# An encoder kernel's opening rewritten: gain row spread by a matmul, dummy products, a hand-pinned order of the first norm tiles

## The chip, the cores and the metric

One core of a Trainium2 chip runs the whole program. The metric is the device time of one execution in microseconds; lower is better. Three runs of the kernel before gave 1115.28, 1116.11 and 1116.93 us (median 1116.11 us).

## The reference, cut to what matters

One encoder layer is applied to two sequences of 512 tokens, each with 16 shared meta tokens ahead of it, in float32. What matters here is its beginning:

```python
hn = _rms(h, attn_norm_g[i])            # x * rsqrt(mean(x*x) + EPS) * g, over 1024 channels
z = hn @ w_in[i]
c_val, c_gate, cq, ckv, k_rope = jnp.split(z, ...)      # 512, 512, 256, 256, 32 columns
u = c_val * jax.nn.sigmoid(c_gate)
u = _depthwise_conv(u, conv_dw_w[i], conv_dw_b[i])      # 31 taps, 512 channels
u = jax.nn.silu(_layernorm(u, conv_ln_g[i], conv_ln_b[i]))
...
# o: attention of 8 heads over latent queries and keys
h = h + jnp.concatenate([u, o], axis=-1) @ w_out[i]
hf = _rms(h, ffn_norm_g[i])
h = h + (jax.nn.silu(hf @ w_gate[i]) * (hf @ w_up[i])) @ w_down[i]
return _rms(h, final_norm_g)[:, N_META:]
```

## The kernel before, in words

Both sequences share one matrix of 1040 token columns: 512 of the first sequence, 16 meta tokens, 512 of the second. The tokens come in nine tiles (`TOK`): tiles 0 to 3 and 5 to 8 of 128 tokens, tile 4 of the 16 meta tokens.

Every large product is made of three passes over operands split into a high and a low part (`fp32r`): high by high, high by low, low by high, added in one PSUM bank (`mm3`, L151). So each weight tile of 128 x 1024 (`pair`) is loaded into a buffer `raw` (two buffers), cast to its high part on ScalarE (L134), and its low part is made by a subtraction on GpSimd (L137). Only when that subtraction is done can `raw` be loaded again.

A norm tile (`norm_tile`) goes this way: the load of `x` (L230, four buffers); the sum of squares on ScalarE (L175); the factor `rs` in two small operations on GpSimd (L176, L177); `xn = x * rs * gain` on VectorE (L237), where `gain` is a tile of 128 equal rows that one transfer of 512 KB has filled (L168); eight transposes on TensorE (L240); the high part `hn_h` by a cast on ScalarE (L141) and the low part `hn_l` by a subtraction on VectorE (L142).

The input product is done by channel blocks of 128. For the convolution's block c (`g0` to `g3`) a gate tile and a value tile of weights are needed: `glu_gate` makes a sigmoid into a `slots` row (L271), `glu_val` multiplies into `U` (L279, L281). Block 0 is done in four column groups (`FIRST`: 256, 272, 256 and 256 columns) as the norm tiles come; the others follow in three groups (`GROUPS`: 512, 272 and 256), in the order of `STEPS`: `g1 c0 g2 c1 g3 c2 q c3 k r n`. A `c` is the convolution of a block: some taps are done by ScalarE and GpSimd (L305, L307), the rest is two chains of operations on VectorE (L322 to L343). `q` and `k` are the latent queries and keys (sums of squares L385, L380, L406, L407), `r` the rotary keys (L436, L437; its table `rope_t` is loaded in L428), `n` the norm of the latent keys (L414, L418). Attention follows, then the output product, the norm and the feed-forward part.

The order on each engine is written out by a scheduler ahead of the run: it gives each engine, in a simulated time, the instruction that is ready and stands earliest in the program. On the chip each engine's instructions start in that order. `tc.keep_in_program_order(ins)` binds an instruction behind the one that stands just before it in the program on the same engine; this is an order of issue, not a wait for the end. The kernel before uses it for some operations of the feed-forward part alone. TensorE's results go to four one-bank buffers (`bank`, tag `t`) and two two-bank buffers (tag `s`).

Of the kernel before, what the change touches and what calls it, by code (L numbers as in the profile page):

```python
# [12 lines left out]
F32 = mybir.dt.float32  # L13
F32R = mybir.dt.float32r
AF = mybir.ActivationFunctionType
# [54 lines left out]
AHEAD = 3  # L70
STEPS = "g1 c0 g2 c1 g3 c2 q c3 k r n"
V_LATE = 1
# [28 lines left out]
def encoder_kernel(ctx: ExitStack, tc: tile.TileContext, x, meta, gains, w_in, w_kr, small, conv_w, wq, wk, wv,  # L101
# [10 lines left out]
    def name(p):  # L112
        n_tile[0] += 1
        return f"{p}_{n_tile[0]}"
# [12 lines left out]
    def pair(src, pool=None, tag="pair", bufs=4):  # L127

        pool = pool or stream
        raw = stream.tile([P, 1024], F32, tag="raw", bufs=2, name=name("raw"))  # L130
        nc.sync.dma_start(raw, src)
        both = pool.tile([P, 2, 1024], F32R, tag=tag, bufs=bufs, name=name("wp"))
        hi, lo = both[:, 0, :], both[:, 1, :]
        nc.scalar.copy(hi, raw)  # L134
        for a in range(0, 1024, LO_W):
            a = slice(a, a + LO_W)
            nc.gpsimd.tensor_sub(lo[:, a], raw[:, a], hi[:, a].bitcast(F32))  # L137
        return hi, lo

    def split(hi, lo, src, src_lo=None):  # L140
        nc.scalar.copy(hi, src)  # L141
        nc.vector.tensor_sub(lo, src_lo if src_lo is not None else src, hi.bitcast(F32))  # L142
# [18 lines left out]
    nc.vector.memset(mhalf, -0.5)  # L161
    nc.scalar.activation(tiny[:, 1:2], ones, AF.Square)
    gq, gkv = sm[:, 0:2], sm[:, 2:4]
    conv_b = sm[:, 4:8]
    ln_g, ln_b = sm[:, 8:12], sm[:, 12:16]
    def gain(i):
        g = const.tile([P, D], F32, tag="gain", bufs=1, name=name("gain"))
        nc.sync.dma_start(g, gains[i:i + 1, :].partition_broadcast(P))  # L168
        return g

    def rms_scale(src, rows, junk):
# [26 lines left out]
             "k": lambda c: [2 * NCH + KL, 2 * NCH + KL + 1], "r": lambda c: [-1]}  # L198
    for step in ("g0 " + STEPS).split():
# [32 lines left out]

    def norm_tile(t, xt):
        col, rows = TOK[t]
        xn = start.tile([P, D], F32, tag="xn", bufs=3, name=name("xn"))
        rs = rms_scale(xt[:rows], rows, start.tile([P, D], F32, tag="junk", bufs=1, name=name("junk")))
        nc.vector.scalar_tensor_tensor(xn[:rows], xt[:rows], rs[:rows], g_attn[:rows], ALU.mult, ALU.mult)  # L237
        pt = psum.tile([P, KD, 128], F32, tag="s", bufs=2, name=name("px"))
        for k in range(KD):
            nc.tensor.transpose(pt[:, k, :rows], xn[:rows, k * 128:(k + 1) * 128], ident[:rows, :rows])  # L240
        split(hn_h[:, :, col:col + rows], hn_l[:, :, col:col + rows], pt[:, :, :rows])

# [3 lines left out]

    def in_proj(i, c0, n):
        pt = bank()
        wh, wl = loaded[i]
        k128 = [slice(k * 128, (k + 1) * 128) for k in range(KD)]  # L250
# [17 lines left out]

    def glu_gate(c, c0, n):
        pg = in_proj(first_of[f"g{c}"], c0, n)  # L270
        nc.scalar.activation(slot(c % 2)[:, c0:c0 + n], pg[:, :n], AF.Sigmoid)  # L271

    def glu_val(c, c0, n):
        sig = slot(c % 2)
        pv = in_proj(first_of[f"g{c}"] + 1, c0, n)
        if True:
# [91 lines left out]
    start_pool.__exit__(None, None, None)  # L368
# [55 lines left out]
    def rope_keys(_):  # L424

        load_w_in(first_of["r"] + AHEAD)
        rope_t = taps.tile([P, NCOL], F32, name="rope_t")
        nc.sync.dma_start(rope_t, rope_k)  # L428
        wb = loaded[first_of["r"]]
# [572 lines left out]

    def in_order(ins):
        tc.keep_in_program_order(ins)

    def g_sums(p, j):
# [321 lines left out]
```

## Time and profile before

| | |
|---|---|
| median of three runs | 1116.11 us (1115.28 to 1116.93) |
| the profiled execution | 1116.52 us, its span 1114.7 us |
| TensorE busy | 1073.9 us (96%) |
| VectorE busy | 835.2 us (75%) |
| ScalarE busy | 500.0 us (45%) |
| GpSimd busy | 472.8 us (42%) |
| DMA | 147.06 MB, mean 132 GB/s |

The shares are averages over the whole span. For a change in the first part, the tables of short stretches, the instructions in order of time and the chain of work that ended last are to be read: they say which engine is full in which stretch, and what the next step waited for. In the rows of instructions in order of time the columns are the start in us, the length in us, engine, line, operation, output and inputs, and how many were merged; in brackets stands the idle time of that engine ahead of it and what ended it.

### The profile page before, as it was taken

The numbers are of one execution on the slowest core, as the hardware profiler recorded it, in microseconds if no ns is written. First come the engines' busy times: TensorE is split into PE (matmuls) and PEld (weight loads), VectorE is DVE, ScalarE is ACT, GpSimd is POOL, SyncE is SP. The second block draws the span as 40 slices with busy tenths as digits, with TensorE's granted clock in tenths as the row PEclk, the third lists the DMA queues.
The fourth block names the chain that finished last, engine by engine and source line by source line (L and its number), as shares of the span: only waits on it lengthen the run. The fifth ranks groups of instructions, "written<-read, shape, count | busy, mean of one in ns | idle before, by whom it ended". The sixth has DMA issues, their size and how long they took to land.

```text
span 1114.7 us, 15902 instructions
## 1 busy us (share of the span) xinstructions
PE 1073.9 (96%) x5874; PEld 928.4 (83%) x5874; DVE 835.2 (75%) x1197; ACT 500.0 (45%) x832; POOL 472.8 (42%) x409
## 2 busy tenths in 40 slices
PE   4999999899998999979999999999999999999997
PEld 4998887788887999968888888888888888888886
DVE  5599997788887555999768767876787596557643
ACT  6455434777785453552232223233323354433331
POOL 6389735654553231576555544554555200000012
PEclk9999999999999999989999999999999999999999
DMA  8211111110100412324354345435543899865503
GB/s 280 71 55 38 48 39 60 39 33 26 39 21 19 171 41 93 114 95 158 135 201 158 119 164 191 168 103 191 187 152 106 277 335 348 288 204 174 182 26 129
DMA packets 71421, 147.06 MB, mean 132 GB/s; under 512 B 6944, under 2 KB 29728, under 8 KB 71344
## 3 DMA queue, kind: packets, MB, share of 16 engines
q1 hardware_dynamic: 71344, 146.06, 38.4%
q8 instruction: 46, 0.75, 0.3%
q14 instruction: 31, 0.25, 0.1%
HBM read 105.92 MB, written 40.11 MB: 131 GB/s over the span
## 4 chain that ended last, share of the span: by engine, by line
PE 77%; DVE 16%; ACT 3%; DMA 1%; issue 1%; POOL 1%; SPq 0%; POOLq 0%; ACTq 0%; DVEq 0%
PE pt L151 58%; PE ps L151 13%; DVE ps L329 3%; DVE ps L337 3%; PE pt L645 3%; PE pt L615 2%; DVE pacc L339 1%; DVE hf L879 1%; PE px L240 1%; DVE wc L964 1%; ACT p L587 1%; DVE act_l L898 1%; DMA raw<-in_w_in_dram 1%; DVE tt L946 0%; DVE cq_l L142 0%
## 5 line engine op out<-in xcount | busy, mean ns | idle before, releaser
L151 PE MATMUL pt<-act_h,wc 128*128 128x512 f32 (+1 forms) x552 | 176.2, 382 | 0.1
L964 POOL TENSOR_TENSOR wc<-tt,wc 128x512 fp32r<-128x512 f32 x84 | 117.7, 1417 | 106.6 <-ACT wc L962 60.0
L151 PE MATMUL pt<-hn_h,wp 128*128 128x256 f32 (+2 forms) x576 | 132.4, 323 | 1.1 <-ACT hn_h L141 1.1
L151 PEld LDWEIGHTS pt<-act_h,wc 128*128 128x128 f32 x552 | 103.4, 190 | 19.8 <-issue 0.3
L176 POOL TENSOR_SCALAR ms<-ms 128x1 f32<-128x1 f32 (+1 forms) x24 | 13.2, 552 | 249.9 <-ACT re L175 213.8
L151 PE MATMUL pt<-act_l,wc 128*128 128x512 f32 (+1 forms) x276 | 105.6, 383 | 3.7 <-DVE act_l L898 3.4
L151 PEld LDWEIGHTS pt<-hn_h,wp 128*128 128x128 f32 x576 | 97.0, 191 | 10.1 <-ACT hn_h L141 1.5
L962 ACT CAST wc<-tt 128x512 fp32r<-128x512 f32 x88 | 51.3, 617 | 118.6 <-PE pt L151 115.3
L1133 DVE TENSOR_TENSOR re<-re,re 128x1024 fp32r<-128x1024 f32 x53 | 63.9, 1222 | 45.0 <-ACT re L1132 43.5
L151 PE MATMUL pt<-hn_l,wp 128*128 128x256 f32 (+2 forms) x288 | 93.5, 325 | 0.0
L137 POOL TENSOR_TENSOR wp<-raw,wp 128x1024 fp32r<-128x1024 f32 x28 | 69.3, 2476 | 54.4 <-ACT wp L134 54.3
L1132 ACT CAST re<-re 128x1024 fp32r<-128x1024 f32 x53 | 54.9, 1054 | 67.9 <-PE pt L151 24.7
L151 PE MATMUL pt<-re 128*128 128x512 f32 x360 | 84.0, 389 | 0.0
L151 PEld LDWEIGHTS pt<-re 128*128 128x128 f32 x360 | 67.6, 188 | 14.0
L590 POOL TENSOR_SCALAR p<-p,sst 128x512 f32<-128x512 f32 x64 | 44.3, 698 | 68.8 <-DVE sst L588 60.9
L151 PE MATMUL pt<-wp,act_h 128*128 128x256 f32 x384 | 71.4, 285 | 1.6 <-DVE h L842 1.5
L151 PEld LDWEIGHTS pt<-act_l,wc 128*128 128x128 f32 x276 | 52.4, 190 | 13.9 <-DVE act_l L898 3.6
L151 PE MATMUL ps<-re 128*128 128x512 f32 x276 | 63.9, 389 | 0.0
L964 POOL TENSOR_TENSOR wc<-raw,wc 128x512 fp32r<-128x512 f32 x30 | 40.3, 1357 | 52.6 <-ACT wc L962 52.6
L151 PEld LDWEIGHTS pt<-wp,act_h 128*128 128x128 f32 x384 | 60.1, 192 | 2.1 <-DVE h L842 1.7
L307 POOL TENSOR_TENSOR pacc<-pacc,prod 128x512 f32<-128x512 f32 x43 | 58.3, 1356 | 7.0 <-ACT prod L305 4.3
L151 PEld LDWEIGHTS ps<-re 128*128 128x128 f32 x276 | 51.8, 188 | 10.7
(283 smaller groups left out, 2889.5 us busy)
## 6 DMA issues: line engine op xcount, KB each, us to landing
raw<-in_w_gate_dram SPq DMA_DIRECT2D x22, 512.0 KB, 4.3
hf<-in_w_down_dram SPq DMA_DIRECT2D x44, 256.0 KB, 4.0
re<-in_w_down_dram SPq DMA_DIRECT2D x31, 256.0 KB, 5.3
raw<-in_w_in_dram SPq DMA_DIRECT2D x12, 512.0 KB, 3.9
slots<-in_w_up_dram SPq DMA_DIRECT2D x11, 512.0 KB, 3.5
h<-in_w_up_dram SPq DMA_DIRECT2D x11, 512.0 KB, 5.6
d_t1t<-hf SPq DMA_DIRECT2D x22, 256.0 KB, 5.5
d_t4t<-hf SPq DMA_DIRECT2D x22, 256.0 KB, 2.5
```

Of the source, the lines that this page charges most:

```text
L137: nc.gpsimd.tensor_sub(lo[:, a], raw[:, a], hi[:, a].bitcast(F32))
L151: nc.tensor.matmul(out_ap, lhsT=w_, rhs=m_, start=first and i + j == 0, stop=last and i == n - 1 and j == 2)
L307: nc.gpsimd.tensor_add(acc, acc, to)
L329: nc.vector.scalar_tensor_tensor(a_, half_win(c, 0, i, HS + 1), k, a_, ALU.mult, ALU.add)
L337: nc.vector.scalar_tensor_tensor(m_, both[:, :, i:i + HS], k, m_, ALU.mult, ALU.add)
L590: nc.gpsimd.tensor_scalar(pr[:, real], pr[:, real], st[:, 2, t:t + 1], 1.0, op0=ALU.mult, op1=ALU.mult)
L615: nc.tensor.transpose(pt[:, t * 128:(t + 1) * 128], self.ps[t][:, n0:n0 + w], ident)
L645: nc.tensor.matmul(self.po, lhsT=v, rhs=p_, start=self.done + j == 1, stop=self.done + j == 5)
L962: nc.scalar.copy(w[:, 0:512], src)
L964: lo_eng.tensor_sub(w[:, 512:1024], src, w[:, 0:512].bitcast(F32))
L1132: nc.scalar.copy(w[:, :, LO], blocks[n])
L1133: nc.vector.tensor_sub(w[:, :, HI], blocks[n], w[:, :, LO].bitcast(F32))
```

## The change: what it does

- **The gain row.** `gain(0)` with its transfer of 512 KB is gone for the first norm. One row of 4 KB is loaded (`g_row`), and two products of 512 columns with a row of ones as weights spread it over 128 partitions into two PSUM banks (`g_attn`). They stay there until the last norm tile. `xn` is made in two halves of 512 columns that read the gain there.
- **Dummy products.** A tile of zeros is multiplied by itself into a bank that nobody reads: 10 products of 256 columns ahead of the gain's two, 31 after them, 6 before and 6 after the transposes of tile 1 (`WARM`).
- **Order.** `norm_tile` becomes a class `Norm` with the stages scale, norm, turn, high and low. For tiles 0 to 4 they are written out one by one, each bound behind the instruction before it on its engine. The two first weight tiles are loaded ahead (`raw_load`), and their casts are bound between the stages. The loads of the later gains and of `rope_t` are bound in program order.
- **Passes.** The first gate and value groups (block 0, columns 0 to 255) run pass by pass: eight high-by-high products, then eight with `hn_l`, then eight with the weights' low part.
- **Block 1 begins earlier.** Its first 256 columns stand behind tile 4 and ahead of block 0's second group in the program; the rest of it (272 and 512 columns) stands behind block 0's last.
- **Small.** ScalarE's first activation is a sigmoid instead of a square; the two `mask` sums read `foldt` during attention instead of `ident`.

```diff
-STEPS = "g1 c0 g2 c1 g3 c2 q c3 k r n"
+STEPS = "c0 g2 c1 g3 c2 q c3 k r n"
+WARM = (10, 31, 6, 6)
...
+    def pair_split(raw, pool=None, tag="pair", bufs=4, pin=lambda ins: ins):
...
-        nc.scalar.copy(hi, raw)
+        pin(nc.scalar.copy(hi, raw))
...
-    nc.scalar.activation(tiny[:, 1:2], ones, AF.Square)
+    nc.scalar.activation(tiny[:, 1:2], ones, AF.Sigmoid)
...
+    def in_order(ins):
+        tc.keep_in_program_order(ins)
+        return ins
+
     def gain(i):
         g = const.tile([P, D], F32, tag="gain", bufs=1, name=name("gain"))
-        nc.sync.dma_start(g, gains[i:i + 1, :].partition_broadcast(P))
+        in_order(nc.sync.dma_start(g, gains[i:i + 1, :].partition_broadcast(P)))
...
+    class Norm:
+        def __init__(self, t, pin=in_order):
+            self.t, self.pin = t, pin
+            self.xt = load_x(t)
+        def scale(self):
...
+            self.pin(nc.scalar.activation(junk[:rows], self.xt[:rows], AF.Square, scale=1.0 / math.sqrt(D),
+                                          accum_out=ms[:rows]))
+            nc.gpsimd.tensor_scalar(ms[:rows], ms[:rows], EPS, 0.0, op0=ALU.add, op1=ALU.add)
+            nc.gpsimd.tensor_tensor(self.rs[:rows], ms[:rows], mhalf[:rows, 0:1], op=ALU.pow)
+        def norm(self):
...
+            for i in range(2):
+                h = slice(i * 512, (i + 1) * 512)
+                self.pin(nc.vector.scalar_tensor_tensor(self.xn[:rows, h], self.xt[:rows, h], self.rs[:rows],
+                                                        g_attn[i][:rows], ALU.mult, ALU.mult))
+        def turn(self):
...
+        def high(self):
...
+        def low(self):
...
+        def all(self):
...
+        if by_pass:
+            three = ((wh, hn_h), (wh, hn_l), (wl, hn_h))
+            for j, (w_, m_) in enumerate(three):
+                for k in range(KD):
+                    in_order(nc.tensor.matmul(pt[:, :n], lhsT=w_[:, k * 128:(k + 1) * 128], rhs=m_[:, k, c0:c0 + n],
+                                              start=j + k == 0, stop=j == 2 and k == KD - 1))
+            return pt
...
-    xs = [load_x(0)]
-    g_attn = gain(0)
+    zero = start.tile([P, 384], F32R, name="zero")
+    nc.vector.memset(zero.bitcast(F32), 0.0)
+    g_row = start.tile([1, D + P], F32, name="g_row")
+    nc.vector.memset(g_row[:, D:], 1.0)
+    n0 = Norm(0)
+    nc.sync.dma_start(g_row[:, 0:D], gains[0:1, :])
     nc.sync.dma_start(ident, eye)
-    xs.append(load_x(1))
-    norm_tile(0, xs[0])
-    load_w_in(0)
-    norm_tile(1, xs[1])
-    xs.append(load_x(2))
-    load_w_in(1)
-    norm_tile(2, xs[2])
+    n1 = Norm(1)
+    raws = [raw_load(w_in[w_order[i]]) for i in range(2)]
+    warm = bank()
+    def warm_up(n):
+        for i in range(n):
+            in_order(nc.tensor.matmul(warm[:, 0:256], lhsT=zero[:, 0:128], rhs=zero[:, 128:384], start=True,
+                                      stop=True))
+    warm_up(WARM[0])
+    g_attn = [bank() for _ in range(2)]
+    for i in range(2):
+        in_order(nc.tensor.matmul(g_attn[i], lhsT=g_row[:, D:], rhs=g_row[:, i * 512:(i + 1) * 512], start=True,
+                                  stop=True))
+    warm_up(WARM[1])
+    n0.scale()
+    n0.norm()
+    n0.turn()
+    n1.scale()
+    n1.norm()
+    n0.high()
+    warm_up(WARM[2])
+    n1.turn()
+    loaded[0] = pair_split(raws[0], pin=in_order)
+    n0.low()
+    n1.high()
+    n1.low()
+    warm_up(WARM[3])
+    loaded[1] = pair_split(raws[1], pin=in_order)
+    n2, n3 = Norm(2), Norm(3)
     nc.sync.dma_start(sm, small)
     nc.sync.dma_start(cw, conv_w)
+    glu_gate(0, *FIRST[0], by_pass=True)
+    n2.scale()
+    n3.scale()
+    glu_val(0, *FIRST[0], by_pass=True)
+    n2.norm()
+    n3.norm()
+    n4 = Norm(4)
+    load_w_in(3)
+    n2.turn()
+    n2.high()
+    n2.low()
+    n3.turn()
+    n3.high()
+    n3.low()
+    n4.all()
...
-    for (c0, n), ahead in zip(FIRST, ((3, 4), (5, 6), (7, 8), ())):
+    glu_gate(1, *FIRST[0])
+    glu_val(1, *FIRST[0])
+    for i, ahead in ((1, (5, 6)), (2, (7, 8)), (3, ())):
         for t in ahead:
-            norm_tile(t, load_x(t))
-        glu_gate(0, c0, n)
-        glu_val(0, c0, n)
-        if len(ahead) == 2:
-            load_w_in(3)
+            Norm(t, pin=lambda ins: ins).all()
+        glu_gate(0, *FIRST[i])
+        glu_val(0, *FIRST[i])
+    for f in (glu_gate, glu_val):
+        for (c0, n) in ((256, 272), (528, 512)):
+            f(1, c0, n)
...
-        nc.sync.dma_start(rope_t, rope_k)
+        in_order(nc.sync.dma_start(rope_t, rope_k))
...
-            nc.vector.tensor_reduce(mask[:, e:e + 1], ident.rearrange("p (r h k) -> p r h k", r=4, h=2)[:, :, e, :],
-                                    axis=AX.XY, op=ALU.add)
+            nc.vector.tensor_reduce(mask[:, e:e + 1], foldt[:, e * META:(e + 1) * META], axis=AX.X, op=ALU.add)
```

More of the change, by code (lines that the diff above doesn't have):

```diff
@@ L198, in encoder_kernel @@
              "k": lambda c: [2 * NCH + KL, 2 * NCH + KL + 1], "r": lambda c: [-1]}
-    for step in ("g0 " + STEPS).split():
+    for step in ("g0 g1 " + STEPS).split():
         if step[0] in tiles:
@@ L243, in encoder_kernel, with in_proj @@
     nc.gpsimd.memset(U[:, :, :, 0:HALO], 0.0)
     nc.gpsimd.memset(U[:, :, :, HALO + LEN:UW], 0.0)
-    def in_proj(i, c0, n):
+    def in_proj(i, c0, n, by_pass=False):
         pt = bank()
         wh, wl = loaded[i]
+        if by_pass:
+            three = ((wh, hn_h), (wh, hn_l), (wl, hn_h))
+            for j, (w_, m_) in enumerate(three):
+                for k in range(KD):
+                    in_order(nc.tensor.matmul(pt[:, :n], lhsT=w_[:, k * 128:(k + 1) * 128], rhs=m_[:, k, c0:c0 + n],
+                                              start=j + k == 0, stop=j == 2 and k == KD - 1))
+            return pt
@@ L1000, in encoder_kernel @@
     units = [Unit(u) for u in range(NFF)]
-    def in_order(ins):
-        tc.keep_in_program_order(ins)
     def g_sums(p, j):
```

42 lines of the change are left out of this document (29 added, 13 removed).

## The prediction, on record before the changed kernel ran

> **What bounds the kernel now.** First the chain of work that ended last, whole and from the start.
>
> ```profile
> span 1114.7 us, 15902 instructions
> PE 77%; DVE 16%; ACT 3%; DMA 1%; issue 1%; POOL 1%; SPq 0%; POOLq 0%; ACTq 0%; DVEq 0%
> 2.58 6.74 DMA raw<-in_w_in_dram
> 10.46 3.34 POOL wp L137
> 15.18 3.37 DVE xn L237
> 18.68 1.94 PE px L240 x8
> 27.94 0.59 PE px L240 x8
> 29.41 0.87 PE px L240 x8
> 175.13 1.67 POOL tiny L407
> 176.85 2.56 PE pt L414 x18
> 179.41 0.89 PE pt L481 x8
> 181.20 2.77 PE pt L151 x12
> ```
>
> TensorE carries 77% of it, but up to 18.7 us it is loads, a cast, GpSimd and VectorE. In between lies a stretch with both engines full, as the stretches of 20 us show (columns: stretch, length, then busy us of PE, PEld, DVE, ACT, POOL).
>
> ```profile
> 80.00:100.00 20.00, 20.00 (x128) 18.11 (x127) 20.00 (x32) 9.98 (x15) 18.00 (x12) 1.00 0.09 27
> 180.00:200.00 20.00, 18.02 (x95) 14.54 (x94) 13.52 (x23) 13.97 (x25) 11.42 (x7) 1.00 0.08 27
> ```
>
> So an earlier start is worth something only if it makes VectorE's convolutions begin earlier, or brings TensorE ahead where VectorE can follow. The next rows (instructions in order of time) show when dense products begin, and the clock by their spacing.
>
> ```profile
> 14.69 0.79 PE L151 MATMUL pt<-hn_h,wp 128*128 128x256 f32 x2 [1.10 <-ACT hn_h L141]
> 15.18 3.36 DVE L237 SCALAR_TENSOR_TENSOR xn<-x,rs,gain 128x1024 f32<-128x1024 f32 x1 [2.48 <-POOL rs L177]
> 18.46 1.21 DVE L142 TENSOR_TENSOR hn_l<-px,hn_h 128x1024 fp32r<-128x1024 f32 x1
> 20.27 0.56 PE L151 MATMUL pt<-hn_l,wp 128*128 128x256 f32 x1
> 20.64 0.63 PE L151 MATMUL pt<-hn_h,wp 128*128 128x256 f32 x2
> 21.27 0.63 PE L151 MATMUL pt<-hn_h,wp 128*128 128x256 f32 x2
> 23.62 0.40 PE L151 MATMUL pt<-hn_h,wp 128*128 128x256 f32 x2
> 25.79 0.39 PE L151 MATMUL pt<-hn_h,wp 128*128 128x256 f32 x2
> 26.14 0.39 PE L151 MATMUL pt<-hn_h,wp 128*128 128x256 f32 x2
> 30.04 0.37 PE L151 MATMUL pt<-hn_l,wp 128*128 128x272 f32 x1
> 50.15 0.42 DVE L279 TENSOR_TENSOR U<-pt,slots 128x256 f32<-128x256 f32 x1 [5.26 <-PE pt L151]
> 52.97 0.74 DVE L329 SCALAR_TENSOR_TENSOR ps<-U,cw,ps 128x514 f32<-128x514 f32 x1
> 53.63 0.74 DVE L337 SCALAR_TENSOR_TENSOR ps<-both,pair_sum,ps 128x512 f32<-128x512 f32 x1
> 176.85 2.56 PE L414 MATMUL pt<-ident,tiny 128*128 128x128 f32 x18 [1.17 <-POOL tiny L407]
> 178.04 3.01 DVE L418 SCALAR_TENSOR_TENSOR slots<-slots,sm,pt 128x512 f32<-128x512 f32 x6 [1.05 <-PE pt L414]
> 187.75 0.69 DVE L568 TENSOR_TENSOR q<-pt,ropeq 128x512 f32<-128x512 f32 x1 [3.16 <-POOL ql L570]
> ```
>
> The first two products run at 14.69 us; then TensorE stands, because `hn_l` of tile 1 is behind tile 2's `xn` on VectorE. Dense work begins at 20.27 us, at 0.63/3 = 0.21 us a product of 256 columns, by 23.62 us the step has shortened, and from 25.79 us it is 0.35/3 = 0.117 us (the granted clock reads 1.00 throughout, so the clock is told here by spacing). Block 0's second group starts at 30.04 us, its `U` is complete at 50.15 us, and then VectorE has its convolutions until TensorE waits 1.17 us for the key norm at 176.85 us. Both engines come out there together; that is where the sum is made.
>
> **The change part by part, up to the first products.**
>
> ```profile
> 0.83 0.07 DVE L161 MEMSET tiny<- 128x9 f32 x1
> 1.17 0.42 SPq L168 DMA_DIRECT2D gain<-in_gains_dram  x1
> 6.92 0.43 SPq L428 DMA_DIRECT2D rope_t<-in_rope_k_dram  x1
> 4.32 1.06 ACT L175 ACTIVATE junk<-x 128x1024 f32<-128x1024 f32 x1 [2.11 <-DMA x<-in_x_dram]
> 5.87 0.57 POOL L177 TENSOR_TENSOR rs<-ms,tiny 128x1 f32<-128x1 f32 x1
> 10.36 1.01 ACT L141 CAST hn_h<-px 128x1024 fp32r<-128x1024 f32 x1
> 15.11 2.35 POOL L137 TENSOR_TENSOR wp<-raw,wp 128x1024 fp32r<-128x1024 f32 x1
> 23.68 1.28 ACT L271 ACT_TABLE_LOAD   x1
> 7.00:8.00 1.00, 0.00 (x0) 0.00 (x0) 1.00 (x2) 0.00 (x0) 0.00 (x0) 1.00 1.03 418
> raw<-in_w_in_dram SPq DMA_DIRECT2D x12, 512.0 KB, 3.9
> ```
>
> - *Gain row.* 512 KB of transfer leave the queue ahead of tile 1 and the weights, and `rope_t` no longer floats up; at the 418 GB/s of 7 to 8 us that is 1.3 us earlier for each load behind. `xn` now has a PSUM operand: two halves at the 0.66 us step of the convolution rows (52.97 to 53.63) are 1.3 us, as those rows keep that step beside a full GpSimd, while the old form took 3.36 us beside the subtraction of 2.35 us. Tile 0 has its factor at 6.44 us as before.
> - *Spreading products.* The four fp32 products of 128 columns at 179.41 took 0.89 us, so one of 512 costs 0.9 us warm, some 1.8 cold. They wait for a 4 KB load issued behind `x`, which lands at 4.32; I take 4.4 us. With 31 dummies behind them in the same queue the transposes of tile 0 start between 4.4 + 1.8 + 3.6 = 9.8 us (all warm) and 4.4 + 3.6 + 6.6 = 14.6 us (all cold). I take 11.0, nearer the warm end, as products needed 3.4 us from 20.27 to the faster step at 23.62, and the ten dummies already count from some 1.3 us on (an estimate: VectorE's last small memset ends at 0.90, then comes that of the zeros). `xn` of tile 0 would be there at 8.4 us: the dummies, not the data, set this end.
> - *First products.* ScalarE's order is now high 0, cast 0, high 1, cast 1: 11.9 + four steps of some 1.02 us gives `hn_h` of tile 1 at 15.0 and cast 1 at 16.0; GpSimd's two subtractions end at 16.4 and 18.8; VectorE's `hn_l` at 16.2. So the passes run at 15.0 to 15.9, 16.2 to 17.1, 17.1 to 18.0, and the value's end at 20.7 us. The table load of 1.28 us goes with the early sigmoid.
> - *Tiles 2 to 4.* `scale` of tile 2 is bound behind the gate's sigmoid, so it starts at 18.4 and not at 16.0. High 2 is bound behind the cast of the fourth weight tile. That tile needs `raw` free (18.8) and a load of 4 us (3.9 from issue to landing in the list of DMA issues): cast at 22.8 to 23.9, highs 2 and 3 to 25.9, tile 4's square and factor (2.1, as 4.32 to 6.44), `xn` (1.3), transposes (0.6) and casts (some 0.7, an estimate for its 16 rows) to 30.6. Block 0's second group starts at 30.9 us: 0.9 us later than before.
> - *What fills that wait.* Block 1's first 256 columns: 48 x 0.117 = 5.6 us, with weights ready at 24.3 and 26.7 us, so they run from 24 to 30 us. That is the change's real yield: TensorE's queue is 5.6 us further, less the 0.9 of the later start, less 0.87 for tile 5's transposes, which before lie ahead of 30.04: 3.9 us ahead.
> - *Begin of the convolutions.* Behind 30.9 us remain 96 products of 0.117, 48 of 272 columns at 0.117 x 272/256 = 0.124 and four tiles' transposes of 0.87: 20.7 us. `U` of block 0 is complete at 51.6 us, against 50.15: VectorE starts some 1.4 us later.
> - *Edits costed at nothing.* The pinned `gain` loads of the later norms and the two `mask` sums move to where the engine that they use has room; the gain's two PSUM banks leave two for products, and a bank comes back one group (2.8 us) after it is full. Were that cover gone, each of the eight groups would lose about 0.4 us, the length of a `U` row.
>
> **The sum.** TensorE reaches the key norm 3.9 us earlier. VectorE arrives with 3.9 + 1.4 us of convolution left over, eight steps of 0.66, which no one needs before the output part. It has idle time for them soon: 3.16 us at 187.75 us alone, 6.5 of 20 us in 180 to 200. But its six L418 rows (3.01 us) will share the queue with them, up to 6 x 0.66 = 4 us, of which TensorE covers 0.89 + 2.77 us by L481 and the query products at 181.20. I take 1.0 us lost (0 to 3). Gain 3.9 - 1.0, some 3.0 us: 1116.5 of the profiled execution becomes 1113.5, and 1116.1, the median, 1113.1 us, with a range of its own of 1111.5 to 1115.
>
> **The rivals.**
> (A) *The lead is not used.* VectorE decides at 177 us: its convolutions are in front in its queue, and it starts no earlier. For it: 20.00 of 20.00 us busy at 80 to 100. Against: they need not be done there. Time 1116.1 + 0.3 = 1116.4 us.
> (B) *The front is faster than I lay out.* If the loads and the clock come early (transposes at 9.8) and the fourth weight tile 2 us sooner, block 0's second group starts at some 27.5 us. Then convolutions begin 2 us earlier as well, and TensorE leads by 7.3: gain 6, 1110 us.
> (C) *Slower, by one order in TensorE's queue.* If tile 4's transposes stand ahead of block 1's first products, TensorE idles from 24 to 29.3 us, and the 5.6 us come afterwards and ahead of block 0's second group. The convolutions then begin at 57 us, 6 later, with no lead: 1121 us. It decides as soon as more than some 4 us of those products fall behind the transposes. For it: the order is made from simulated times, which need not know a load of 4 us. Against: the products' weights are loaded early in the program.
> (D) *The clock is not up when the dummies run.* If the ten dummies' 2.1 us and the pause until 4.4 do not count, half of the 31 run at 0.21: transposes at 12.9, everything behind 1.9 us later, lead 2, convolutions 3.3 later: 1116 us.
> The Trainium skill, page "TensorE: Matmul & The Clock Gate", Part 1, says that the clock rises after a busy window of about 3.4 us, counted in a window that does not start with the kernel. By that rule (D) is what a badly placed window would give; the trace agrees so far that the step shortens 3.4 us after 20.27 us.
>
> **How the numbers follow.** No change is what lies within 0.2% (2.2 us) of 1116.1, about what a measurement of this kernel can tell: 1113.9 to 1118.3. The likeliest case has 0.45, and five parts in six of it are faster than that. (A) has 0.18, (B) 0.18, (C) 0.10 and (D) 0.09. Faster: 0.37 + 0.18 = 0.55; slower: (C), a fifth of (A) and (D) and a bit of a new order later in the program, 0.18; same: 0.27. The range reaches from 1108.5, short of (B)'s far end, to 1118.5, past (A) and (D) and short of (C).
>
> **What would show it.** In the changed trace: dummies from some 1.3 us and products at 0.117 us from the first pass on; transposes of tile 0 at 11 us behind the dummies, with `xn` long done; `xn` halves of 0.66 us beside a busy GpSimd; high 2 waiting for the cast of the fourth weight tile; block 1's products between 24 and 30 us; the first L322 at 52 us; L414 near 173 us and L337 rows behind it. The prediction is wrong if L322 starts well before 49 us or after 55 us, or if L414 still stands at 177 us.

## The result and the profile after

The changed kernel takes 1129.37 us (median of four runs, 1127.69 to 1132.85), the kernel before 1115.69 us (median of four, three of them those given ahead of the prediction). The ratio is 1.0122, 95% interval 1.0104 to 1.0140: 1.2% slower. 1113.1 us had been predicted, 1118.5 us at most. The profiled execution took 1130.19 us, 13.7 us more than that of before. In a later run, e16, one of twelve executions took 2758.89 us, and e16's median in the table below is that of the other eleven.

The first two lines of the page, then stretches (columns as in the prediction, then PEclk, the granted clock of TensorE, DMA share and GB/s):

```profile
span 1128.4 us, 16021 instructions
PE 1089.8 (97%) x5931; PEld 942.2 (83%) x5931; DVE 832.2 (74%) x1208; ACT 498.3 (44%) x831; POOL 466.7 (41%) x409
0.00:20.00 20.00, 17.16 (x82) 13.94 (x83) 5.96 (x10) 7.61 (x10) 4.94 (x14) 1.00 0.59 194
20.00:40.00 20.00, 15.44 (x104) 14.77 (x103) 5.67 (x8) 7.86 (x12) 8.66 (x8) 0.83 0.50 158
40.00:60.00 20.00, 17.96 (x131) 17.73 (x132) 12.35 (x18) 9.31 (x16) 3.91 (x10) 0.83 0.09 27
28.00:32.00 4.00, 3.79 (x17) 3.79 (x18) 0.07 (x1) 1.17 (x2) 3.73 (x4) 0.50 0.76 253
44.00:48.00 4.00, 4.00 (x21) 3.91 (x20) 2.55 (x5) 2.07 (x4) 1.29 (x3) 0.51 0.28 111
```

VectorE, ScalarE and GpSimd work no longer than before; TensorE has 15.9 us more. The 53 dummies and the gain's products are part of that, products at half clock another: 28 to 32 and 44 to 48 us are busy at a clock of 0.50, where the kernel before, from 24 to 64 us, has 1.00 in every stretch of 4 us. The first 60 us in order of time, on TensorE:

```profile
1.36 2.50 PE L415 MATMUL pt<-zero 128*128 128x256 f32 x10 [1.36 <-DVE zero L403]
4.64 3.75 PE L422 MATMUL pt<-g_row 1*128 1x512 f32 x4 [0.77 <-DMA g_row<-in_gains_dram]
8.32 6.38 PE L415 MATMUL pt<-zero 128*128 128x256 f32 x31
14.54 1.03 PE L274 MATMUL px<-ident,xn 128*128 128x128 f32 x8
18.53 1.22 PE L304 MATMUL pt<-hn_h,wp 128*128 128x256 f32 x8 [0.67 <-ACT hn_h L279]
26.57 0.60 PE L274 MATMUL px<-ident,xn 128*128 128x128 f32 x4
28.80 1.06 PE L274 MATMUL px<-ident,xn 128*128 128x128 f32 x4
36.92 1.04 PE L274 MATMUL px<-ident,xn 128*128 128x128 f32 x8
41.89 2.40 PE L274 MATMUL px<-ident,xn 16*128 16x16 f32 x12 [3.94 <-DVE xn L267]
43.94 0.80 PE L160 MATMUL pt<-hn_h,wp 128*128 128x272 f32 x2
```

and on the engines that feed it (the first row is tile 0's factor; then tile 0's high part, tile 2's square, the value's sum with tile 2's factor behind it; GpSimd's subtraction for a weight tile, the second small operation of tile 3 and tile 3's factor; tile 3's high part, tile 4's square, the first convolution):

```profile
8.43 0.75 DVE L267 SCALAR_TENSOR_TENSOR xn<-x,rs,pt 128x512 f32<-128x512 f32 x1 [0.90 <-PE pt L422]
15.61 1.02 ACT L279 CAST hn_h<-px 128x1024 fp32r<-128x1024 f32 x1 [7.00 <-PE px L274]
22.26 1.05 ACT L257 ACTIVATE junk<-x 128x1024 f32<-128x1024 f32 x1
24.87 0.42 DVE L336 TENSOR_TENSOR U<-pt,slots 128x256 f32<-128x256 f32 x1 [5.13 <-PE pt L304]
25.21 1.40 DVE L267 SCALAR_TENSOR_TENSOR xn<-x,rs,pt 128x512 f32<-128x512 f32 x2
29.00 2.37 POOL L146 TENSOR_TENSOR wp<-raw,wp 128x1024 fp32r<-128x1024 f32 x1
31.33 0.57 POOL L260 TENSOR_TENSOR rs<-ms,tiny 128x1 f32<-128x1 f32 x1
31.93 1.41 DVE L267 SCALAR_TENSOR_TENSOR xn<-x,rs,pt 128x512 f32<-128x512 f32 x2 [5.32 <-POOL rs L260]
37.99 1.01 ACT L279 CAST hn_h<-px 128x1024 fp32r<-128x1024 f32 x1 [3.07 <-PE px L274]
38.90 1.05 ACT L257 ACTIVATE junk<-x 16x1024 f32<-16x1024 f32 x1
67.08 1.01 DVE L379 TENSOR_TENSOR both<-U 128x542 f32<-128x542 f32 x1
```

The reader is to see four things. Some 25 of the 31 dummies start 0.213 us apart, half clock, and only the last six 0.12 us apart; tile 0's transposes stand behind them, though their `xn` has been ready since 9.2 us, and ScalarE idles 7.00 us for them. VectorE idles 5.13 us for the value's sum, and tile 2's factor is bound behind it. Tile 3's factor then waits another 5.32 us, for its small operations on GpSimd (`rs`, L260), which stand there around the subtraction at 29.00 us; and its transposes come only at 36.92 us, 8 us after tile 2's second half, because 44 products of block 1 stand between them in TensorE's queue (block 1's 256 columns are 48 products; the 88 of e12's expectation counts their weight loads as well). Tile 4's square is bound behind tile 3's high part, so the second group of block 0 starts at 43.94 us (30.04 before) and the first convolution at 67.08 us (50.61 before). A loss of 16.5 us there is 13.7 us at the end.

One more loss lies far behind the edit. In the feed-forward part TensorE waits once for a product sum on VectorE:

```profile
508.82 0.58 PE L160 MATMUL pt<-s4h,wc 128*128 128x256 f32 x1 [3.23 <-DVE h L1081]
```

Before, that wait was 0.94 us.

### The profile page after: what moved, and what is told of

Read it like the earlier page. It is cut to its first block, busy times and chain, and to the rows that moved or that the text cites. A ratio compares the mean times of both kernels' runs of the same rounds, so it can differ in the third digit from the quotient of the medians.

```text
span 1128.4 us, 16021 instructions
## 1 busy us (share of the span) xinstructions
PE 1089.8 (97%) x5931; PEld 942.2 (83%) x5931; DVE 832.2 (74%) x1208; ACT 498.3 (44%) x831; POOL 466.7 (41%) x409
## 4 chain that ended last, share of the span: by engine, by line
PE 77%; DVE 15%; ACT 3%; issue 2%; DMA 1%; POOL 1%; SPq 0%; POOLq 0%; ACTq 0%; DVEq 0%
PE pt L160 58%; PE ps L160 13%; DVE ps L386 3%; PE pt L747 2%; DVE ps L394 2%; PE pt L717 2%; DVE pacc L396 1%; PE px L274 1%; DMA sm<-in_small_dram 1%; DVE hf L981 1%; DVE wc L1066 1%; DVE tt L1048 1%; DVE act_l L1000 1%; ACT p L689 1%; DVE sst L688 0%
## 5 line engine op out<-in xcount | busy, mean ns | idle before, releaser
L160 PE MATMUL pt<-hn_h,wp 128*128 128x256 f32 (+2 forms) x544 | 129.2, 331 | 2.5 <-ACT wp L143 2.5
L189 POOL TENSOR_SCALAR ms<-ms 128x1 f32<-128x1 f32 x15 | 8.4, 559 | 240.8 <-ACT re L188 213.8
L160 PEld LDWEIGHTS pt<-hn_h,wp 128*128 128x128 f32 x544 | 94.1, 195 | 11.5 <-ACT wp L143 2.9
L146 POOL TENSOR_TENSOR wp<-raw,wp 128x1024 fp32r<-128x1024 f32 x28 | 67.3, 2406 | 56.3 <-ACT wp L143 56.2
L160 PE MATMUL pt<-hn_l,wp 128*128 128x256 f32 (+2 forms) x272 | 90.0, 331 | 0.0
L1231 ACT CAST re<-re 128x1024 fp32r<-128x1024 f32 x53 | 55.5, 1053 | 71.4 <-PE pt L160 26.7
L160 PEld LDWEIGHTS pt<-re 128*128 128x128 f32 x360 | 67.6, 188 | 14.0
L160 PE MATMUL pt<-s4h,wc 128*128 128x512 f32 (+1 forms) x184 | 59.6, 387 | 3.2 <-DVE h L1081 3.2
```

Of the source, the lines that this page charges most:

```text
L160: nc.tensor.matmul(out_ap, lhsT=w_, rhs=m_, start=first and i + j == 0, stop=last and i == n - 1 and j == 2)
L1231: nc.scalar.copy(w[:, :, LO], blocks[n])
```

## The experiments

The theory from that profile: (1) the bound order of tiles 2 to 4, (2) the dummies, most of them at half clock, (3) a queue order far behind that flips. Rivals: block 1's place alone, or the gain row. "T4" is the fourth temp of the second feed-forward unit (L946 before, `Unit.temp`). Medians in us; the kernel before lay at 1116.5 to 1117.3 us in these sessions, and ratios are against it. The last two columns are starts in the profiled execution.

| run | median | ratio, 95% interval | second group | first convolution |
|---|---|---|---|---|
| e1 block 1 back | 1127.78 | 1.0101 (1.0086 to 1.0116) | 39.8 | 62.3 |
| e2 tiles 2 to 4 free | 1120.32 | 1.0035 (1.0022 to 1.0047) | 35.6 | 55.5 |
| e3 no dummies | 1123.62 | 1.0070 (1.0046 to 1.0094) | 35.0 | 58.2 |
| e4 gain row only | 1116.54 | 1.0002 (0.9993 to 1.0012) | 26.6 | 47.4 |
| e5 e4 and T4 late | 1113.72 | 0.9975 (0.9966 to 0.9984) | 27.0 | 47.9 |
| e6 before and T4 late | 1116.53 | 0.9998 (0.9989 to 1.0007) | 30.4 | 50.9 |
| e7 after and T4 late | 1126.49 | 1.0089 (1.0075 to 1.0103) | 40.2 | 62.9 |
| e8 e2, no dummies, T4 late | 1115.56 | 0.9990 (0.9979 to 1.0000) | 31.4 | 52.7 |
| e9 e8 with 30 dummies first | 1118.06 | 1.0012 (1.0002 to 1.0022) | 31.3 | 55.7 |
| e10 e5 with 30 dummies first | 1116.21 | 1.0000 (0.9991 to 1.0009) | 29.9 | 50.7 |
| e11 e8 with block 1 back | 1119.01 | 1.0021 (1.0012 to 1.0030) | 28.6 | 53.1 |
| e12 squares first, bound | 1131.04 | 1.0129 (1.0107 to 1.0151) | 42.0 | 67.6 |
| e13 squares and factors first, bound | 1121.33 | 1.0048 (1.0035 to 1.0061) | 37.6 | 57.4 |
| e14 e13, no dummies, T4 late | 1119.17 | 1.0028 (1.0018 to 1.0038) | 36.3 | 56.2 |
| e15 e8 with nothing bound | 1117.63 | 1.0014 (1.0006 to 1.0023) | 33.3 | 54.9 |
| e16 e5 with block 1 early | 1116.20 | 0.9993 (0.9983 to 1.0003) | 33.3 | 53.3 |

**One part taken away, or done alone (e1 to e4).**

```diff
e1  -STEPS = "c0 g2 ..."                    +STEPS = "g1 c0 g2 ..."   (block 1 behind block 0 again)
e2  -n2, n3 = Norm(2), Norm(3)
    +n2, n3 = Norm(2, pin=lambda ins: ins), Norm(3, pin=lambda ins: ins)
    -n4 = Norm(4)
    +n4 = Norm(4, pin=lambda ins: ins)
e3  -WARM = (10, 31, 6, 6)                  +WARM = (0, 0, 0, 0)
e4  before.py, with g_row, its two products and xn in halves; nothing else
```

> The changed kernel with block 1's products back in their old place (three groups behind block 0, not 256 columns ahead of its second group); pins, dummies and the gain row stay. Theory P (place: block 1's products stand among tile 2's transposes and ahead of tile 3's and 4's in TensorE's queue, and that makes block 0's second group late, 43.9 us for 30.0): the second group starts by 34 us and the time falls from 1129 to 1119 us or less. Rival B (binding: ScalarE's bound order, high 2 behind the fourth weight tile's cast and tile 4's square behind high 3, makes it late whatever TensorE has in between): the second group starts at 37 us or later, the time stays at 1123 us or more. Rival D (dummies): no change beyond 2 us.

> The changed kernel with tiles 2, 3 and 4 free of the binding in program order (tiles 0 and 1, the first passes, the dummies and block 1's early products stay). Theory P: tile 4 still stands ahead of block 1's products only if the scheduler puts it there; if it does, block 0's second group starts before 38 us and the time falls below 1122 us; if block 1 stays in front, no change. Rival B: 1119 us or less, with tile 3's transposes no longer at 36.9 us but before 28 us. Rival D: 1129 us within 2.

> The changed kernel without any dummy product (none of 10, 31, 6, 6). Theory D (the 31 dummies ran at half clock, 6.4 us, held tile 0's transposes from 8.4 to 14.5 us, and with them the casts, the weights' low parts and so the loads of the next weight tiles): tile 0's transposes at some 9.5 us, everything behind 4 to 6 us earlier, 1124 us. Theory P or B alone: the front is earlier, but the waits behind it stay, and the first passes run at half clock, 1127 to 1130 us.

> The kernel before with the gain row alone (row of 4 KB, two spreading products, xn in two halves that read PSUM); no dummies, no binding, no passes, old order. If the gain row is good by itself (no 3.4 us xn beside GpSimd, 512 KB less in the queue), dense products begin at 17 to 18.5 us instead of 20.3 and the time is 1113 to 1114.5 us. If VectorE and the scheduler's new order use it up, 1116 us within 1.5. If the two PSUM banks held until tile 8 cost products their buffers, 1118 us or more.

Freeing tiles 2 to 4 gives back 9.0 us: tile 3's transposes start at 24.66 us, as rival B had it, while the time lies just above B's 1119 us and within the bounds of theory P as well. Leaving the dummies out gives back 5.7 us, as theory D said. Putting block 1 back gives 1.6 us, and the second group stays late, as rival B had it. These 1.6 us are not shown to be the worth of block 1's place: the intervals of e1 and of the changed kernel overlap, and e1 does not have the late loss of the next experiments; beside e7, which has block 1 early and that loss mended, e1 is 1.3 us slower by the medians. What e1 does show is that tile 3 is late even with none of block 1's products ahead of it. Its factor waits for GpSimd as in the changed kernel, and its transposes start at 31.83 us:

```profile
31.02 1.41 DVE L267 SCALAR_TENSOR_TENSOR xn<-x,rs,pt 128x512 f32<-128x512 f32 x2 [5.50 <-POOL rs L260]
```

The gain row alone starts the second group 3.5 us earlier than before and the first convolution 3.2 us earlier, and the end does not move: where those 3 us go was the next question.

**The flip far behind (e5 to e7).** VectorE in e4, then the product that waits; and its clock in that stretch:

```profile
493.73 1.75 DVE L953 TENSOR_TENSOR tt<-h,tt 128x512 f32<-128x512 f32 x1
495.41 0.41 DVE L986 TENSOR_TENSOR h<-pt,h 128x256 f32<-128x256 f32 x1
495.87 0.39 PE L151 MATMUL pt<-s4h,wc 128*128 128x256 f32 x1 [3.10 <-DVE h L986]
495.00:500.00 5.00, 4.13 (x18) 3.65 (x19) 4.96 (x9) 2.31 (x5) 5.00 (x4) 0.71 0.30 105
```

The row at 493.73 is T4. In the kernel before it stands behind the sum that frees TensorE's bank, and the wait there is 0.94 us:

```profile
495.84 0.41 DVE L979 TENSOR_TENSOR h<-pt,h 128x256 f32<-128x256 f32 x1
496.18 1.43 DVE L946 TENSOR_TENSOR tt<-h,tt 128x512 f32<-128x512 f32 x1
496.31 0.39 PE L151 MATMUL pt<-s4h,wc 128*128 128x256 f32 x1 [0.94 <-DVE h L979]
```

In e2, e3, e4, e12, e13 and the changed kernel the scheduler's simulated time has turned the two round (waits of 2.6 to 3.3 us at that product), in e1 not (0.92 us). The pause of 3.10 us is followed by products at a mean clock of 0.71. T4 held back, and nothing else:

```diff
-            nc.vector.tensor_sub(self.t[n], x_, y_)
+            ins = nc.vector.tensor_sub(self.t[n], x_, y_)
+            if self.u == 1 and n == "t4":
+                tc.keep_in_program_order(ins)
```

> The kernel before with the gain row spread by a matmul (as in the run that did that alone, 1116.54 us) and the fourth temp of the second feed-forward unit held on VectorE behind the first unit's product sums. Theory A: the gain row brings about 3 us in the front, and about 3 us are lost near 495 us because VectorE takes that temp ahead of a product sum that TensorE's bank waits for; with the temp held back the loss goes and the end is at 1113.0 to 1114.2 us. Theory B: the front's gain dissolves before the attention and the place of the temp is without effect; 1116.0 to 1117.0 us. Row that decides: the pause of TensorE at its first s4h product, 3.10 us in that run and 0.94 us before.

> Control: the kernel before with nothing changed but the fourth temp of the second feed-forward unit held behind the first unit's product sums. There it already stands behind the first of them, and is put two places later. Theory A (the loss is the temp's place ahead of the sum): within 0.1% of 1116.7 us. Theory B (holding the temp back is a gain by itself, whatever the front does): 1113 to 1114.5 us.

> The changed kernel with nothing else than that temp held back. Theory A: the flip of that order is a part of the loss of 13 us, so about 3 us come back: 1125.5 to 1127.5 us. Theory B: 1128.5 to 1130.5 us.

All three came out by theory A. e5 is 2.8 us faster than e4, with a wait of 1.56 us at that product; e6 shows that holding T4 back is worth nothing where it already stands late; in the changed kernel it gives 2.9 us, by the medians. e5 beats both kernels: 1113.72 us.

The single starts in the table are to be read with care where a kernel has dummies. e7 has the changed kernel's code up to the feed-forward part, and yet its profiled execution starts the second group 3.7 us earlier and the first convolution 4.2 us earlier. It has the full clock where the profile of the changed kernel has 0.50:

```profile
28.00:32.00 4.00, 4.00 (x36) 4.00 (x35) 1.01 (x2) 1.40 (x2) 2.93 (x2) 1.00 0.82 241
```

**The state that the prediction assumed (e8, e11).**

```diff
e8   after.py with e2's and e3's edits and T4 held back
e11  e8 with e1's edit
```

> The changed kernel with norm tiles 2 to 4 not bound to the program's order, no dummy products, and the temp held back: what is left of the change is the gain row, the first products pass by pass, the early sigmoid table and block 1's first columns ahead of block 0's second group. It tests whether TensorE's lead by block 1 is worth what the prediction said. If it is (second group no later than 31 us, first convolution no later than 51.6 us): 1112 to 1114 us. If the lead is not used, or the second group still starts late: the second group at 32 to 36 us and 1115.5 to 1119 us; by the slope of the four runs so far (0.9 us of the end for each us of the first convolution's start) a convolution at 54 us gives 1117.5 us less the temp's 3 us.

> As the run with tiles 2 to 4 free, no dummies and the temp held back (1115.56 us; second group 31.4 us, first convolution 52.7 us, the exponential table 193.0 us), with block 1's products put back behind block 0's as before the change. The two differ in TensorE's lead of 5.6 us alone. Theory A (the lead is of use, as the prediction said, about 3 us): without it the first convolution starts at 47 to 49 us but the end is 1116 to 1118.5 us. Theory B (VectorE, busy 10 of 10 us from 60 us on, sets the pace of the convolutions, so an earlier first convolution is worth more than the lead): the end is 1112.5 to 1114.5 us.

e8 has the second group at 31.43 us (30.9 predicted) and the first convolution at 52.69 us (51.6): nearly the predicted front, with TensorE 5.6 us of block 1 further, less 1.4 us for the later group, so 4.2 us ahead of the kernel before. It gains 1.2 us (0 to 2.3 by the interval, so less than the 3.0 predicted), and the second expectation, without a use for the lead, was the nearer one. TensorE's waits in e8 behind 60 us, and its clock there:

```profile
31.43 0.37 PE L160 MATMUL pt<-hn_h,wp 128*128 128x272 f32 x1
52.69 1.01 DVE L379 TENSOR_TENSOR both<-U 128x542 f32<-128x542 f32 x1
138.75 1.05 PE L483 MATMUL pt<-tiny,slots 128*128 128x1 f32 x8 [1.66 <-DVE slots L488]
175.06 4.10 PE L517 MATMUL pt<-ident,tiny 128*128 128x128 f32 x18 [1.79 <-POOL tiny L510]
170.00:180.00 10.00, 8.21 (x55) 7.75 (x53) 10.00 (x22) 1.63 (x2) 4.48 (x3) 0.83 0.33 110
```

The key norm comes at 175.06 us, 1.8 us earlier than the 176.85 of before. The other 2.4 us went for the most part in waits: 1.66 us for VectorE at 138.75 us (0.54 before) and 1.79 us (1.17 before) at 175.06 us, there for GpSimd, which had itself waited for VectorE (L509, at 173.12 us). That is 1.8 us more than before. And behind the second the 18 products take 4.10 us instead of 2.56, at a mean clock of 0.83. The row that opens attention's exponentials then stands at

```profile
193.00 1.28 ACT L689 ACT_TABLE_LOAD   x1
```

against 193.22 us before. Against e11 the lead is worth 3.45 us, somewhat more than theory A's range. But the first convolution does not start at 47 to 49 us in e11, as both theories had it; it starts at 53.1 us, no earlier than in e8. What block 1's products do there is to fill a pause. In e11 the stretches are

```profile
24.00:28.00 4.00, 0.64 (x8) 0.57 (x8) 2.32 (x4) 3.75 (x6) 3.64 (x4) 0.88 0.91 298
28.00:32.00 4.00, 3.04 (x13) 2.75 (x14) 3.33 (x6) 0.75 (x4) 0.81 (x3) 0.50 0.29 117
```

so the pause costs its length and a clock of 0.50 behind it.

**The dummies and the clock (e9, e10).**

```diff
e9   -WARM = (0, 0, 0, 0)  +WARM = (30, 0, 4, 8)     (on e8)
e10  +30 dummy products ahead of the gain's two      (on e5)
```

> The changed kernel with norm tiles 2 to 4 free, the temp held back, and the dummy products otherwise placed: 30 ahead of the gain row's products, none behind them, 4 and 8 ahead of tile 1's transposes and the first passes. It asks what the clock's rise counts. Theory A (only products of full rows count, and some 3 to 7 us of them without a pause are needed): the 30, from 1.36 us on, take about 0.206 us each until the clock rises between 5 and 8 us; the gain products then take 0.4 to 0.5 us each instead of 0.94, tile 0's transposes about 1.03 us instead of 2.0, and tile 0's transposes start at 8 to 10 us at full clock. Theory B (the time since the start decides, or the gain products count too): the dummies and the gain products all run at half clock and the rise is again at 14 us or later. By A the end is 0 to 3 us below the run without dummies (1115.56 us), by B 1 to 4 us above it.

> The kernel before with the gain row's matmul and the temp held back (1113.72 us), and 30 dummy products ahead of the gain products, as a candidate for a version faster than both. Theory A (the clock is up by 8 us): tiles 0 and 1's transposes at 1.03 us for 8 instead of 2.0, the first products at full clock, first convolution 0.5 to 2 us earlier than in that run, the end at 1112 to 1113.5 us. Theory B (it is not, or pauses take the clock down again before the first products): the gain products are pushed back by about 3 us for nothing and the end is at 1114 to 1116.5 us.

```profile
1.36 5.62 PE L415 MATMUL pt<-zero 128*128 128x256 f32 x30 [1.36 <-DVE zero L403]
6.91 1.98 PE L422 MATMUL pt<-g_row 1*128 1x512 f32 x4
17.21 1.94 PE L274 MATMUL px<-ident,xn 128*128 128x128 f32 x8 [4.52 <-DVE hn_l L283]
16.00:20.00 4.00, 2.79 (x13) 2.82 (x14) 3.50 (x4) 4.00 (x7) 3.83 (x4) 0.50 0.78 277
```

On the clock theory A holds: in e9 the dummies start 0.213 us apart up to 5.37 us and about 0.117 us apart from 5.53 us on, so the clock rose some 4.1 us after the first of them, and the gain products behind take 1.98 us instead of 3.75. On the time theory B does: both kernels lose 2.5 us.

In e9 not all of that loss is the clock's. Its scheduled order on ScalarE differs from e8's: the squares of tiles 2 and 3 stand ahead of tile 0's high part, which comes at 13.44 us (9.96 in e8), though its transposes are done by 10.2 us.

```profile
10.98 1.06 ACT L257 ACTIVATE junk<-x 128x1024 f32<-128x1024 f32 x1 [3.18 <-DMA x<-in_x_dram]
```

So TensorE waits 4.52 us, is back at 0.50, and starts the first passes at 18.80 us instead of 13.93. In e10 the gain products are 3.7 us later than in e5. There the clock rises at 7.7 us and is back near half at 11.1 us, although TensorE has no pause between 1.49 and 13.31 us:

```profile
11.00:12.00 1.00, 1.00 (x7) 0.76 (x5) 0.94 (x2) 0.96 (x1) 0.92 (x2) 0.56 1.04 427
```

Ahead of this fall lie the products of one row (8.00 to 9.98 us); that they are its cause is not shown. In both kernels the raised clock was lost before the passes came.

**Which binding (e12 to e15).**

```diff
e12  after.py, n2, n3, n4 = Norm(2), Norm(3), Norm(4) and their scale() moved ahead of n0.high()
e13  e12 with their norm() moved too; n2.turn, high, low between glu_gate and glu_val, n3's behind glu_val
e14  e13 with WARM = (0, 0, 0, 0) and T4 held back
e15  e8 with no pin in Norm and pair_split, by_pass=False
```

> The changed kernel, everything still bound to the program's order and all its dummies, but with that order altered in one thing: the loads, squares and powers of norm tiles 2 to 4 are written ahead of tile 0's high part, so that ScalarE can do the squares in its idle time of 7.00 us while it waits for tile 0's transposes. Theory A (not the binding but the order that is bound, the squares behind sigmoid, casts and high parts, is what costs): tile 3's and 4's transposes by 33 us, second group at 34 to 37 us instead of 43.9, the end at 1119 to 1123 us, near the 1120.32 us of the run with tiles 2 to 4 free. Theory B (it is the place of tile 3's transposes behind 88 products of block 1 on TensorE, whatever the squares): second group after 40 us, 1126 to 1129 us.

> The changed kernel with all its bindings and dummies, the bound order altered: squares, powers and factors of norm tiles 2 to 4 ahead of tile 0's high part, tile 2's transposes and parts between the gate's and the value's passes, tile 3's right behind the value's. Theory A (the place of the factors on VectorE, behind the value's sum, and with it that of the transposes behind block 1's products, is what costs, not the binding): second group at 33 to 37 us, the end at 1118 to 1122 us, as with tiles 2 to 4 free (1120.32 us). Theory B (something else in the binding, the queues' waits in fixed order): second group after 40 us, 1125 to 1130 us.

> The same bound order without the dummy products and with the temp held back: the state that the prediction assumed. If the prediction's sum is right but for the order: second group at 30 to 32 us, first convolution 51 to 53 us, 1112 to 1114.5 us. If a bound order costs by itself beside a free one: 1115 to 1119 us, the free one having given 1115.56 us.

> The changed kernel without dummies and with no stage of any norm tile, no weight cast and no first product bound (the gain products and the gain's load still are), the first products not pass by pass, the temp held back. Theory A (the passes and the binding of tiles 0 and 1 start the first products earlier, at 13.9 us, and are worth 1 to 3 us): 1116.5 to 1119 us. Theory B (they are worth nothing): within 1 us of the 1115.56 us.

My theory on e12 fell. ScalarE did the squares of tiles 2 to 4 by 15.1 us, most of it in its idle time, and nothing came of it (1131.04 us): tile 2's factor stayed bound behind the value's sum, tile 3's transposes (from 33.31 us, with their factor done by 28.63) behind block 1's products, and tile 4's factor (39.41 us) behind tile 3's low part.

```profile
25.58 0.42 DVE L336 TENSOR_TENSOR U<-pt,slots 128x256 f32<-128x256 f32 x1 [5.16 <-PE pt L304]
25.92 2.71 DVE L267 SCALAR_TENSOR_TENSOR xn<-x,rs,pt 128x512 f32<-128x512 f32 x4
```

With the factors ahead of that sum as well (e13), everything still bound, 8.0 of the 9.0 us come back. So binding is not what cost, but the order that was bound: factors and transposes of tiles 2 to 4 behind sums and products that come late. Which of the two cost how much is not separated, as e13 moves both; its second group (37.6 us) lies just outside theory A's 33 to 37. Nor is a bound order a gain by itself: in e14 the squares of tiles 2 to 4, which end at 15.0 us because their loads come late, are bound ahead of tile 0's high part, whose transposes are done at 10.2 us,

```profile
17.90 2.08 PE L304 MATMUL pt<-hn_h,wp 128*128 128x256 f32 x8 [5.93 <-ACT hn_h L279]
```

so the first passes start at 17.90 us instead of e8's 13.93, and the end is 3.6 us above e8, just above the 1115 to 1119 us expected of a bound order. e15 is 2.1 us above e8, by theory A: the passes and the binding of tiles 0 and 1 and of the weight casts, taken away together here, are the one part of the new order that pays, with the other bindings and the dummies away.

**Block 1 where no pause is (e16).** e5 with `g1` early in `STEPS` and block 1's first gate and value behind block 0's.

> The kernel before with the gain row's matmul, the temp held back (together 1113.72 us) and block 1's products of the first 256 columns put behind block 0's first ones, nothing bound. Theory A (TensorE's early work adds what it gave between the two free runs, 3.45 us, less what the first convolution is later): 1111 to 1113 us. Theory B (TensorE has no pauses left there that block 1 could fill, since in that run it is busy from 16.5 us on, and the first convolution comes up to 5.6 us later): 1114 to 1117 us.

Theory B: the same 5.6 us of products that gained 3.45 us in e8 lose 2.5 us here, and the first convolution comes 5.4 us later than in e5:

```profile
47.86 1.01 DVE L324 TENSOR_TENSOR both<-U 128x542 f32<-128x542 f32 x1
53.30 1.01 DVE L324 TENSOR_TENSOR both<-U 128x542 f32<-128x542 f32 x1
```

(e5, then e16).

## Why the prediction was wrong, point by point

- **Gain row: right.** The halves of `xn` take 0.75 us alone and about 0.70 us in pairs (0.66 predicted), and keep that beside GpSimd's subtraction (e8, four halves and the subtraction that they overlap with):

```profile
20.32 2.71 DVE L267 SCALAR_TENSOR_TENSOR xn<-x,rs,pt 128x512 f32<-128x512 f32 x4 [2.18 <-POOL rs L260]
21.71 2.37 POOL L146 TENSOR_TENSOR wp<-raw,wp 128x1024 fp32r<-128x1024 f32 x1
```

  The Trainium skill, page "SBUF — State Buffer", section "Who interferes with whom", says that a VectorE instruction with at most one input in SBUF, outside the modes that use two ports, does not contend with GpSimd; these rows agree. Tile 0's `xn` is there at 9.2 us (8.4), the spreading took 3.75 us from 4.64 us (up to 3.6 from 4.4). It is worth 3 us, which e5 shows.
- **Transposes of tile 0: the wrong value within right bounds.** 9.8 to 14.6 us was given, 11.0 taken, 14.54 measured. The step "the ten dummies already count" failed: neither they nor the gain products brought the clock up, and some 25 of the 31 ran at half clock. That is rival (D), whose mechanism held but which was priced for half of them, at 1.9 us. The 3.4 us to the faster step were also counted from 20.27 us, where the prediction's own chain has TensorE at work on tile 2's transposes from 18.68 us without a pause behind them: 4.8 to 4.9 us, nearer to the 5.5 us measured from the full-row dummies' start to the rise at 13.8 us. The dummies cost 5.7 us in the changed kernel (e3).
- **First products: right in order, late in time.** High 0, cast 0, high 1, cast 1 came in that order, ScalarE's table load was gone, each 3.5 to 4 us later; the value's end at 24.8 us instead of 20.7 is the transposes' delay carried on.
- **Tiles 2 to 4: the step that failed most.** The prediction saw tile 2's square behind the sigmoid (22.26 us here, the mechanism right) and put tile 4's transposes at 30.6 us. The step that failed is "highs 2 and 3 to 25.9": it lets high 3 follow high 2 at once, and so gives tile 3's factor and transposes no time of their own. Measured, high 2 came at 29.90 us and high 3 at 37.99. Of these 8.1 us the first part is the factor: with tile 3's square behind the cast of the third weight tile (26.08 us), and its two small operations around GpSimd's subtraction at 29.00 us, it starts at 31.93 us and ends at 33.34. The rest is TensorE's queue, where 44 products of block 1 hold the transposes until 36.92 us. The value's sum, behind which tile 2's factor is bound, cost less: that factor was ready at 24.35 us and started at 25.21. Tile 4's square, bound behind high 3, came at 38.90 us, the second group at 43.94 instead of 30.9. High 2 itself was late by the dummies' delay carried on (the fourth weight tile's cast at 27.13 us instead of 22.8). Rival (C) looked for trouble in the same queue but the other way round (transposes ahead of the products).
- **Filling the wait: half right.** Block 1's products do fill a pause, worth 3.45 us (e8 against e11). In the changed kernel they fill it in the wrong place, and TensorE idles 3.94 us after them.
- **The sum: mis-sized.** With the assumed front all but reached, a lead of 4.2 us gave 1.2 us at the end (0 to 2.3) instead of 3.0 (e8, by the medians; by the profiled spans, 1114.1 and 1114.7 us, 0.6). The term was "1.0 us lost (0 to 3)". Measured, 2.4 us are gone by the key norm, and 1.6 of the other 1.8 us by the exponentials, in waits for VectorE, for GpSimd behind VectorE, and in products at a lower clock behind them. This is rival (A) for most of the lead.
- **A term that was missing.** The flipped order at 495 us, 2.9 us (e7). The prediction had "a bit of a new order later in the program" among the chances, and no place for it in the sum.

The parts do not add: 9.0 + 5.7 + 2.9 = 17.6 us alone, 13.8 us together (e8), since, it seems, the dummies' delay and the bound order keep the same products waiting. Not tried: the bindings of tiles 3 and 4 one by one, and the changed kernel with its tile 4 ahead of block 1 by a binding on TensorE alone.

## What to carry to other kernels

When instructions are bound to program order, write down for each of them what stands just ahead of it on its own engine, on every engine, and ask when that one can start: a transpose behind another block's products waits for all of them, and a factor waits for the engine that makes its scale. Dummy products paid in none of the three direct comparisons here (the changed kernel and e3, e9 and e8, e10 and e5), although they raised the clock: they stood ahead of work that was ready, or the clock was down again before the real products came. And after any change at the front, compare the queues far behind it: one operation that a scheduler moved ahead of a bank's release took back all of a gain of 3 us, and a binding of one instruction restored it.

## What the runs showed of the hardware

- The products of one row did not raise the clock. In the changed kernel TensorE had no pause from 4.64 us on, and products are at full rate only from 13.8 us on: 9.2 us after the gain products' start, 5.5 us after that of the full-row dummies. With 30 dummies first it rose 4.1 us (e9) and 6.2 us (e10) after their start. The Trainium skill, page "TensorE: Matmul & The Clock Gate", Part 1, says that the rise follows a full busy window of about 3.4 us that runs free of the kernel; an estimate worked out from this figure is a rise 3.4 to 6.8 us after the start. The 5.5, 4.1 and 6.2 us agree, and had the gain products counted, 4.64 + 6.8 = 11.4 us would have been the latest. That the single row is the reason is argued, not shown: these products differ from the dummies in type and width too (though in e3, with no dummies, the clock was up at the first passes, 13.07 us, behind fp32 transposes of 128 rows).
- How much of a pause lowers it differed from run to run. The single pause of 3.10 us at 495 us in e4 left a mean clock of 0.71 over 495 to 500 us, while 1.56 us at the same place in e5 cost nothing. Two pauses of 1.46 and 1.05 us ahead of 28.80 us in the changed kernel left 0.50 over 28 to 32 us, while e7, with the same code there and pauses of 1.16 and 1.04 us, has 1.00. In e10 the clock was near half again at 11.1 us with no pause of TensorE since 1.49 us.
